# A state-space stage whose causal convolution of x runs with tokens on the partitions

## The chip, the cores and the metric

One core of one Trainium2 chip runs the whole program as a single launch. The metric is device time in microseconds (us); lower is better. The engines are TensorE (PE, with its weight loads PEld), VectorE (DVE), ScalarE (ACT), GpSimd (POOL) and SyncE (SP); copies run on 16 DMA engines. SBUF and PSUM tiles have 128 partitions.

## What is computed

The reference is a two-layer decoder trunk over 256 tokens of width 2048: latent attention, a squared-ReLU MLP, a Mamba-2 state-space mixer, and a second MLP. Everything is float32. Only the mixer is changed. Cut to what matters:

```python
zxbcdt = h @ w_in                                  # 256 x 10304
z, xbc, dt = split(zxbcdt, [4096, 4096 + 6144])    # xbc = x (4096) | B (1024) | C (1024)
xbc = silu(causal_depthwise_conv(xbc, conv_w, conv_b))   # 4 taps along the tokens, per channel
xs, b_in, c_in = split(xbc, [4096, 5120])          # 8 groups x 8 heads x 64 | 8 x 128 | 8 x 128
y = ssd_chunked_scan(xs, softplus(dt + dt_bias), a, b_in, c_in)   # one chunk of 256 tokens
y = (y + d_skip * xs) * silu(z)
y = y * rsqrt(mean(y * y over the group) + eps) * norm_g
x = x + y @ w_out
```

The convolution is out[s] = b + w3 v[s] + w2 v[s-1] + w1 v[s-2] + w0 v[s-3] for each channel, with zeros ahead of token 0.

## The kernel before

Every large product is float32 split in two halves. A unit of weights, 128 x 1024, is loaded into `wraw` by SP (six buffers). ACT copies it, rounded, to `wh` (`halves`, L103) and DVE subtracts to `wl` (L104), four buffers each. The products of a unit are 12 matmuls of 128 x 512 (`products`, L362 to L364). The loads run six units ahead of the products and the splits three (`flow.ahead`), so the split of unit j+4 needs the buffers that unit j gives up.

`ssm_plan` lists the units of the state-space stage in the order of `SSM_ORDER`. A step is a block of x, z, B or C: 8 units, whose result is 256 tokens x 512 channels in two PSUM banks with the tokens on the partitions. An output step "o" is 4 units for each of its four column blocks. TensorE's order is exactly the order in which the program text issues its instructions. On the other engines a list scheduler chooses the order. Small work between the units is timed by a clock in the code: `when(us, fn)` puts a function in a list, and `move(us)` advances the clock by 2.72 a unit and runs what is due; `small` also keeps such pieces apart.

x blocks 0 to 7 are the 8 head groups. `x_done` handles a finished one. `evac` copies its two banks to SBUF on ACT, scaled by the norm factor (L1117). `conv` then works in two halves of 256 channels. Four transposes (L1128) put the channels on the partitions and the tokens along the free axis. ACT forms tap 3 and the bias (L1135), DVE adds the other taps as shifted reads of the same PSUM bank, six instructions per half (L1138), and ACT applies Silu (L1139). `back` transposes the result to tokens on partitions again (L1257, twice four transposes per group), ACT copies it to `xtm` (L1260), and DVE, POOL and `across` prepare the operands of the chunk product: `xd` = x dt, a copy weighted by the decay to the chunk's middle (`xh`, `xl`), and x times the skip factor. `heads(g)` loads the decay rows (`cm`), takes exponentials and issues the group's 32 + 32 small matmuls in `product`. `gate` multiplies with silu(z), normalises and transposes (`turn`) to `yT`, which the output steps read. B and C blocks go through the same `conv` and stay with channels on the partitions.

DMAs are issued by SP, which processes its list in order, and by ACT where the code says `nc.scalar.dma_start`. A DMA that ACT issues stands in ACT's instruction order.

Of the kernel before, what the change touches and what calls it, by code (L numbers as in the profile page):

```python
# [20 lines left out]
F32 = mybir.dt.float32  # L21
# [3 lines left out]
ALU = mybir.AluOpType  # L25
# [205 lines left out]
class Trunk:  # L231
# [849 lines left out]
    def ssm_body(self, sp, dp, gain):  # L1081
# [16 lines left out]
        def small(us, fn, gap=2.6):  # L1098
            at[1] = max(at[0] + us, at[1] + gap)
            when(at[1] - at[0], fn)  # L1100
# [8 lines left out]
        heads_of = lambda v: v.rearrange("p (h f) -> p h f", h=8)  # L1109
        spread = lambda v, g: v[:, 8 * g:8 * g + 8].unsqueeze(2).to_broadcast([P, 8, 64])  # L1110
        diagonal = lambda: cst[:, C_TRI:C_TRI + P]

        def evac(accs):
            ev = []
            for t in range(2):
                e = self.scratch()
                nc.scalar.activation(e, accs[t], AF.Copy, scale=rs[t])  # L1117
                ev.append(e)
            return ev
# [38 lines left out]
        def cb_group(g):  # L1158
            B, C = fm["B", g // 4][:, g % 4], fm["C", g // 4][:, g % 4]
            b = self.ps(self.sm, "sm")  # L1160
            nc.tensor.matmul(b[:, 0:256], B[:, 0:P], C, start=True, stop=True)
            nc.tensor.matmul(b[:, 256:384], B[:, P:256], C[:, P:256], start=True, stop=True)
            at[0] += 0.65
            t = sp.tile([P, 2, P], F32, name=f"cb{g}")
            far[g] = sp.tile([P, 2, P], F32R, name=f"cf{g}")
            for i in range(2):
                nc.vector.tensor_tensor(t[:, i], b[:, 2 * i * P:2 * i * P + P], diagonal(), ALU.mult)
            self.split_out(far[g][:, 0], far[g][:, 1], b[:, P:256])
            cb[g] = t
# [20 lines left out]
        def dt_chain(b):  # L1190
# [50 lines left out]

            small(15, cums)

        def x_done(g, accs):
            fmx = [None, None]
            ev = evac(accs)
            xg[g], xd[g] = [None, None], [None, None]

            def dst(j, a):
                fmx[j] = a  # L1250
                return a

            def back(t):
                b = self.ps(self.sm, "sm")
                for k in range(4):
                    o = (k % 2) * 256 + t * P
                    nc.tensor.transpose(b[:, k * P:(k + 1) * P], fmx[k // 2][:, o:o + P], self.ident)  # L1257
                at[0] += 0.45
                x = sp.tile([P, 512], F32, tag="xtm", name=f"xtm{g}_{t}", bufs=XTM)
                nc.scalar.activation(x, b, AF.Copy)  # L1260
                w = sp.tile([P, 512], F32, tag="xd", name=f"xd{g}_{t}", bufs=XD)
                nc.vector.tensor_tensor(heads_of(w), heads_of(x), spread(dt[:, t], g), ALU.mult)
                xg[g][t], xd[g][t] = x, w
                if t == 0:
                    xw = self.scratch()
                    nc.gpsimd.tensor_tensor(heads_of(xw), heads_of(x), spread(edge[:, 0], g), ALU.mult)
                    xh = sp.tile([P, 512], F32R, tag="xh", name=f"xh{g}", bufs=1)
                    xl = self.s2.tile([P, 512], F32R, tag="s2", name=self.name("s2"))
                    self.split_out(xh, xl, xw)
                    small(8, lambda: across(xh, xl))  # L1270
                nc.gpsimd.tensor_tensor(heads_of(x), heads_of(x), spread(cst[:, C_DSK:C_DSK + 64], g), ALU.mult)
                if t:
                    waiting.append(g)
                    if len(waiting) == 1:
                        heads(g)

            def across(xh, xl):
                b = self.ps(self.sm, "sm")
                nc.tensor.matmul(b, far[g][:, 0], xh, start=True, stop=False)
                nc.tensor.matmul(b, far[g][:, 1], xh, start=False, stop=False)  # L1280
                nc.tensor.matmul(b, far[g][:, 0], xl, start=False, stop=True)
                at[0] += 0.7
                w = self.scratch()
                nc.vector.tensor_tensor(heads_of(w), heads_of(b), spread(edge[:, 1], g), ALU.mult)
                nc.gpsimd.tensor_tensor(xg[g][1], xg[g][1], w, ALU.add)

            def after():
                small(10, lambda: back(0))
                small(10, lambda: back(1))

            conv(ev, 4 * g, dst, after)

        def heads(g):

            cm = []
            for i in range(4):
                m = sp.tile([P, 2, 2, P], F32, tag="cm", name=f"cm{g}_{i}", bufs=4)
                nc.sync.dma_start(m.rearrange("p a t n -> p (a t n)"), cumD[4 * g + i:4 * g + i + 1].to_broadcast([P, 2 * S]))
                cm.append(m)

            def exponent(i):
                for k in range(2):
                    for t in range(2):
                        h = 8 * g + 2 * i + k
                        nc.scalar.activation(cm[i][:, k, t], cm[i][:, k, t], AF.Relu, bias=cumT[:, t, h:h + 1], scale=-1.0)

            def decay():
                for m in cm:
                    nc.scalar.activation(m, m, AF.Exp, scale=-1.0)
                scores = cb[g][:, 0:2].rearrange("p t n -> p (t n)").unsqueeze(1).to_broadcast([P, 2, 2 * P])  # L1310
                for m in cm:
                    v = m.rearrange("p a t n -> p a (t n)")
                    nc.vector.tensor_tensor(v, v, scores, ALU.mult)
                small(10, product)

            def product():
                y = [self.ps(self.yp, "y") for t in range(2)]
                for t in range(2):
                    for i in range(8):
                        o = slice(i * 64, (i + 1) * 64)  # L1320
                        for r in (slice(0, 64), slice(64, 128)):
                            nc.tensor.matmul(y[t][r, o], cm[i // 2][:, i % 2, t, r], xd[g][t][:, o], start=True, stop=True)
                at[0] += 1.8
                at[1] = max(at[1], at[0])
                for t in range(2):
                    nc.vector.tensor_tensor(xg[g][t], xg[g][t], y[t], ALU.add)
                waiting.pop(0)
                if waiting:
                    heads(waiting[0])

                def done():
                    ready.add(g)
                    gate(g)

                when(2, done)

            begin = 24 if g == 1 else 0
            for i in range(4):
                when(begin + 3 + 2.2 * i, lambda i=i: exponent(i))
            when(begin + 11, decay)  # L1340
# [9 lines left out]
        def gate(g):  # L1350
            if g not in ready or g not in ws:
                return
            ng = self.gain_tile(d["sng"][g])
            ssq = self.stat(2)
            for t in range(2):
                x = xg[g][t]
                nc.gpsimd.tensor_tensor(x, ws[g][t], x, ALU.mult)
                self.square_sum(x, ssq[:, t:t + 1])
            r = self.rsqrt(ssq, 2, 512)
            yT[g] = (self.ktile(self.k4), self.ktile(self.k4))  # L1360
            for t in range(2):
                nc.vector.scalar_tensor_tensor(ws[g][t], xg[g][t], r[:, t:t + 1], ng, ALU.mult, ALU.mult)

            def turn(t):
                sl = slice(t * P, (t + 1) * P)
                b = self.ps(self.sm, "sm")
                for j in range(4):
                    nc.tensor.transpose(b[:, j * P:(j + 1) * P], ws[g][t][:, j * P:(j + 1) * P], self.ident)
                at[0] += 0.45
                self.split_out(yT[g][0][:, :, sl], yT[g][1][:, :, sl], b.rearrange("p (k n) -> p k n", k=4))  # L1370

            lag = 14 if g == 1 else 10
            small(lag, lambda: turn(0))
            small(lag, lambda: turn(1))
            small(lag + 2, lambda: gated.add(g))

        done = {"B": lambda i, a: bc_done("B", i, a), "C": lambda i, a: bc_done("C", i, a), "x": x_done, "z": z_done}
        accs = None
        for tok in ssm_plan():
# [40 lines left out]


XTM, XD = 6, 4


def ssm_plan():
    out = []
    for step in SSM_ORDER:
# [7 lines left out]
        else:  # L1435
# [2 lines left out]


X_AT = (1, 2, 3, 3)  # L1440
SSM_ORDER = ["B0", "dt0", "C0", "x0", "x1", "B1", "C1", "z0", "z1", "x2", "x3", "o0", "z2", "z3", "x4", "x5", "o1",
             "z4", "z5", "x6", "x7", "o201", "z6", "z7", "o223"]


B12 = "raw"
# [195 lines left out]
```

## Time and profile before

| | |
|---|---|
| median of 3 runs | 2306.25 us (2305.49 to 2308.09) |
| profiled execution, its own time | 2306.98 us |
| its span, first to last instruction | 2305.2 us |
| PE, DVE, ACT, POOL busy | 2294.9, 1854.1, 1432.4, 182.7 us |
| granted TensorE clock, mean | 1.000 |
| state-space stage, projections and scan | about 957 to 1581 us of the span |
| in that stretch of 624 us: PE, DVE, ACT busy | 623.62, 428.15, 386.35 us |
| in that stretch: DMA engines' share, rate | 0.61, 192 GB/s |

PE's busy time is the union of its matmuls, which overlap; one unit of 12 matmuls takes 2.72 us from start to start. In rows of groups the columns are: source line, engine, operation, output <- inputs, shape, count | busy us, mean ns of one | idle us of the engine ahead of it and what ended that.

### The profile page before, as it was taken

Reading aid. Unit: us, or ns where it says so; the run is one execution under the profiler, and the core shown is the slowest. Engines: PE = TensorE matmul, PEld = TensorE weight load, DVE = VectorE, ACT = ScalarE, POOL = GpSimd, SP = SyncE. Lnnn points to the kernel's source line nnn. Section 1 sums busy time; section 2 is a strip of 40 time slices with the busy share of each in tenths; the row PEclk is TensorE's granted clock in tenths of the full one; section 3 lists DMA queues with packets and bytes.
Section 4 is the critical chain, followed back from the end, with each engine's and each line's share of the span. In section 5 each row is a group of like instructions: output and inputs, shape, how many; then the busy total and the mean of one; then the engine's idle time right before and its main releaser. Section 6 shows DMA issues by size and latency. Waiting matters only on the chain.

```text
span 2305.2 us, 30566 instructions
## 1 busy us (share of the span) xinstructions
PE 2294.9 (100%) x11065; PEld 1905.9 (83%) x11065; DVE 1854.1 (80%) x2180; ACT 1432.4 (62%) x1986; POOL 182.7 (8%) x223
## 2 busy tenths in 40 slices
PE   9999999999999999999999999999999999999999
PEld 7888888888888888888888888888888888888887
DVE  7776697999899897677677676766989889889895
ACT  7775465566666656576656566565666656666663
POOL 1430000000000000001010111110000000000000
PEclk9999999999999999999999999999999999999999
DMA  8444687887887877655566656566687788787874
GB/s 320 146 132 151 205 233 240 265 240 247 265 244 248 267 215 241 197 184 182 187 198 193 207 177 214 187 193 201 203 260 231 251 266 249 239 270 240 250 229 161
DMA packets 146102, 508.68 MB, mean 221 GB/s; under 512 B 16480, under 2 KB 17184, under 8 KB 145952
## 3 DMA queue, kind: packets, MB, share of 16 engines
q1 hardware_dynamic: 137664, 477.30, 62.8%
q0 software_dynamic: 8064, 29.36, 7.7%
q8 instruction: 87, 1.43, 0.2%
q14 instruction: 63, 0.52, 0.1%
q10 hardware_dynamic: 224, 0.07, 0.0%
HBM read 504.51 MB, written 2.16 MB: 220 GB/s over the span
## 4 chain that ended last, share of the span: by engine, by line
PE 97%; issue 1%; DVE 1%; DMA 0%; ACT 0%; POOL 0%; SPq 0%; DVEq 0%; ACTq 0%; POOLq 0%
PE yp L363 9%; PE yp L364 9%; PE yp L362 9%; PE acc L362 8%; PE acc L364 8%; PE acc L363 8%; PE st L363 8%; PE st L364 8%; PE st L362 8%; PE acc L345 3%; PE acc L341 3%; PE acc L342 3%; PE sm L326 2%; PE a L341 1%; PE kv L341 1%
## 5 line engine op out<-in xcount | busy, mean ns | idle before, releaser
L104 DVE TENSOR_TENSOR wl<-wraw,wh 128x1024 fp32r<-128x1024 f32 (+2 forms) x818 | 991.6, 1226 | 307.3 <-ACT wh L103 298.0
L103 ACT ACTIVATE wh<-wraw 128x1024 fp32r<-128x1024 f32 (+2 forms) x818 | 858.0, 1053 | 574.8 <-PE yp L364 178.2
L363 PE MATMUL yp<-wl,k 128*128 128x512 f32 x896 | 348.9, 389 | 1.0 <-DVE wl L104 1.0
L362 PE MATMUL yp<-wh,k 128*128 128x512 f32 x896 | 349.8, 390 | 0.0
L364 PE MATMUL yp<-wh,k 128*128 128x512 f32 x896 | 348.8, 389 | 0.0
L362 PE MATMUL acc<-wh,xt 128*128 128x512 f32 x704 | 279.3, 397 | 0.0
L363 PE MATMUL acc<-wl,xt 128*128 128x512 f32 x704 | 274.4, 390 | 0.4 <-DVE wl L104 0.4
L364 PE MATMUL acc<-wh,xt 128*128 128x512 f32 x704 | 274.7, 390 | 0.0
L103 ACT ACTIVATE wh<-wrx 128x1024 fp32r<-128x1024 f32 x168 | 177.9, 1059 | 136.4 <-PE yp L364 109.5
L104 DVE TENSOR_TENSOR wl<-wrx,wh 128x1024 fp32r<-128x1024 f32 x168 | 204.0, 1220 | 36.6 <-ACT wh L103 36.3
L363 PEld LDWEIGHTS yp<-wl,k 128*128 128x128 f32 x896 | 168.3, 188 | 36.3 <-DVE wl L104 1.9
L364 PEld LDWEIGHTS yp<-wh,k 128*128 128x128 f32 x896 | 168.2, 188 | 35.0
L362 PEld LDWEIGHTS yp<-wh,k 128*128 128x128 f32 x896 | 168.3, 188 | 34.6
L362 PE MATMUL st<-wh,xt 128*128 128x512 f32 x448 | 176.8, 395 | 0.0
L363 PE MATMUL st<-wl,xt 128*128 128x512 f32 x448 | 174.8, 390 | 0.0
L364 PE MATMUL st<-wh,xt 128*128 128x512 f32 x448 | 174.8, 390 | 0.0
L364 PEld LDWEIGHTS acc<-wh,xt 128*128 128x128 f32 x704 | 132.1, 188 | 28.1
L363 PEld LDWEIGHTS acc<-wl,xt 128*128 128x128 f32 x704 | 132.4, 188 | 27.1 <-DVE wl L104 1.2
L362 PEld LDWEIGHTS acc<-wh,xt 128*128 128x128 f32 x704 | 132.3, 188 | 26.1 <-issue 0.2
L199 POOL DMA_DIRECT2D wrx<-mi x56 | 49.0, 876 | 1140.8 <-DVE wl L104 988.6
L362 PE MATMUL st<-wh,sN 128*128 128x512 f32 x336 | 132.3, 394 | 0.0
L364 PE MATMUL st<-wh,sN 128*128 128x512 f32 x336 | 130.9, 390 | 0.0
(318 smaller groups left out, 3558.4 us busy)
## 6 DMA issues: line engine op xcount, KB each, us to landing
wraw<-mi SPq DMA_DIRECT2D x256, 512.0 KB, 5.2
wraw<-mo SPq DMA_DIRECT2D x256, 512.0 KB, 5.2
wraw<-si SPq DMA_DIRECT2D x160, 512.0 KB, 4.4
wraw<-so SPq DMA_DIRECT2D x64, 512.0 KB, 4.1
wrx<-mi SPq DMA_DIRECT2D x56, 512.0 KB, 5.0
wrx<-mi POOLq DMA_DIRECT2D x56, 512.0 KB, 8.0
wraw<-wo SPq DMA_DIRECT2D x32, 512.0 KB, 3.9
wraw<-ukv SPq DMA_DIRECT2D x16, 512.0 KB, 4.5
```

The lines of the kernel that those rows point to most:

```text
L103: self.last = nc.scalar.activation(h[:, v], raw[:, v], AF.Copy)
L104: nc.vector.tensor_tensor(lo[:, v], raw[:, v], h[:, v].bitcast(F32), ALU.subtract)
L199: nc.gpsimd.dma_start(st["b11"].tile, quarter(d, 1, 0), accum_op=ALU.add)
L326: self.nc.tensor.transpose(b[:, j * P:(j + 1) * P], src[:, j * P:(j + 1) * P], self.ident)
L341: nc.tensor.matmul(accs[t][:, :n], ah, wh[:, q, :], start=first and kt + q == 0, stop=False)
L342: nc.tensor.matmul(accs[t][:, :n], al, wh[:, q, :], start=False, stop=False)
L345: nc.tensor.matmul(accs[t][:, :n], lhs(kt + q, t)[0], wl[:, q, :], start=False, stop=en and q == nk - 1)
L362: nc.tensor.matmul(b, ah, wh, start=first and q == 0, stop=False)
L363: nc.tensor.matmul(b, ah, wl, start=False, stop=False)
L364: nc.tensor.matmul(b, al, wh, start=False, stop=last and q == 1)
```

## The change

B and C keep the old way. For x there are no transposes. `x_begin` copies a finished block into one tile `ev` (partitions = tokens, two token halves, 512 channels). For each half of 256 channels `shifted` issues six DMAs from ACT. For a shift m = 1, 2, 3 one copies 128 - m partitions of both token halves to `ex`, m partitions lower, and a second copies the m partitions that cross from the first 128 tokens to the second. `weighted` then runs on DVE: all three shifted copies times their taps in one 128 x 1536 instruction, and five 128 x 512 instructions for the unshifted tap, the bias and the sums. ACT's Silu writes `xtm`. The taps come as rows broadcast over the partitions (`cx`, one buffer, 640 KB, SP queue, 16 loads). `ev` and `ex` exist once, so the halves of all groups run one after the other through `line`; `LAG` holds the code's clock distances. `finish` does what `back` did after its copy. The order of the blocks is new, the special delays of group 1 are gone, the `cf` tiles share six buffers, and the SBUF scratch of software DMAs is 1024 bytes instead of 4096.

```diff
+        ex, ev, tap = sp.tile([P, 3, 2, 256], F32, name="ex"), sp.tile([P, 2, 512], F32, name="ev"), {}
+        line = []
+        nc.gpsimd.memset(ex[0:3, :, 0], 0.0)
...
-            far[g] = sp.tile([P, 2, P], F32R, name=f"cf{g}")
+            far[g] = sp.tile([P, 2, P], F32R, tag="cf", name=f"cf{g}", bufs=6)
...
+        def taps(k):
+            if k < 2 * GROUPS:
+                w = sp.tile([P, 5, 256], F32, tag="cx", name=f"cx{k}", bufs=1)
+                nc.sync.dma_start(w.rearrange("p a n -> p (a n)"), d["cx"][k:k + 1].to_broadcast([P, 5 * 256]))
+                tap[k] = w
+
         def x_done(g, accs):
-            ev = evac(accs)
...
-            def back(t):
-                    nc.tensor.transpose(b[:, k * P:(k + 1) * P], fmx[k // 2][:, o:o + P], self.ident)
...
-            conv(ev, 4 * g, dst, after)
+            line.append((g, accs))
+            if len(line) == 1:
+                x_begin(g, accs)
+
+        def x_begin(g, accs):
+            for t in range(2):
+                nc.scalar.activation(ev[:, t], accs[t], AF.Copy, scale=rs[t])
+
+            def shifted(j):
+                v = ev[:, :, j * 256:(j + 1) * 256]
+                for m in range(1, 4):
+                    nc.scalar.dma_start(ex[m:, m - 1], v[:P - m])
+                    nc.scalar.dma_start(ex[:m, m - 1, 1], v[P - m:, 0])
+                when(LAG[0], lambda: weighted(j))
+
+            def weighted(j):
...
+                def one():
+                    tt(ex, ex, w[:, 1:4].unsqueeze(2).to_broadcast([P, 3, 2, 256]), ALU.mult)
+                def two():
+                    tt(v, v, both(0), ALU.mult)
+                    tt(v, v, both(4), ALU.add)
+                def three():
+                    taps(2 * g + j + 1)
+                    tt(ex[:, 0], ex[:, 0], ex[:, 1], ALU.add)
+                    tt(v, v, ex[:, 2], ALU.add)
+                def four():
+                    tt(v, v, ex[:, 0], ALU.add)
+                    for t in range(2):
...
+                        nc.scalar.activation(xg[g][t][:, j * 256:(j + 1) * 256], v[:, t], AF.Silu)
+                    if j == 0:
+                        when(LAG[1], lambda: shifted(1))
+                    else:
+                        when(LAG[2], finish)
+                        line.pop(0)
+                        if line:
+                            x_begin(*line[0])
+
+                for i, fn in enumerate((one, two, three, four)):
+                    when(LAG[4] * i, fn)
...
-            begin = 24 if g == 1 else 0
+            begin = 0
...
-            lag = 14 if g == 1 else 10
+            lag = 10
...
+LAG = (6,0,8,14,2.6)
...
-SSM_ORDER = ["B0", "dt0", "C0", "x0", "x1", "B1", "C1", "z0", "z1", "x2", "x3", "o0", "z2", "z3", "x4", "x5", "o1",
-             "z4", "z5", "x6", "x7", "o201", "z6", "z7", "o223"]
+SSM_ORDER = ["B0", "dt0", "C0", "x0", "z0", "x1", "z1", "B1", "x2", "C1", "o001", "x3", "o023", "z2", "x4", "z3", "x5", "o101", "z4", "x6", "z5", "x7", "o123", "z6", "o201", "z7", "o223"]
...
-    nc = bacc.Bacc("TRN2", target_bir_lowering=False, num_devices=1, dynamic_dma_scratch_size=4096)
+    nc = bacc.Bacc("TRN2", target_bir_lowering=False, num_devices=1, dynamic_dma_scratch_size=1024)
```

How the change moves instructions shows best at x block 0. In rows of an order, a name's last number is the tile's running number, and the brackets list the semaphores that the instruction waits for (DMAHW0 to DMAHW7 are set by DMAs, which share these eight).

ACT before, from the end of x block 0: the two copies out of PSUM, the next weight split, and other work until the transposed half is ready.

```order
L1117 ACTIVATE s_688_9384<-acc_9165,rs_160 128x512 [waits PE_49]
L1117 ACTIVATE s_689_9386<-acc_9166,rs_160 128x512 [waits PE_49]
L103 ACTIVATE wh_9401<-wraw_9303 128x1024 [waits DMAHW5_49]
L315 ACTIVATE cf_9392<-sm_9388 128x128 [waits DVE_49,PE_49]
L1305 ACTIVATE cm_1_9583<-cm_1_9583,cumT 128x128
```

ACT now at the same place:

```order
L1261 ACTIVATE ev<-acc_9170,rs_160 128x512 [waits PE_49]
L1261 ACTIVATE ev<-acc_9171,rs_160 128x512 [waits PE_49]
L1267 DMA ex<-ev 1x16x16 [waits DMAHW5_49,Activation_49]
L1266 DMA ex<-ev 127x2x256 [waits DMAHW6_49,Activation_49]
L1266 DMA ex<-ev 126x2x256 [waits DMAHW7_49]
L1267 DMA ex<-ev 2x256 [waits DMAHW0_49]
L1266 DMA ex<-ev 125x2x256 [waits DMAHW1_49]
L1267 DMA ex<-ev 3x256 [waits DMAHW2_49]
L315 ACTIVATE cf_9401<-sm_9397 128x128 [waits DVE_49,PE_49]
L103 ACTIVATE wh_9410<-wraw_9308 128x1024
L103 ACTIVATE wh_9429<-wraw_9335 128x1024 [waits PE_49]
```

Six DMAs now stand between the copies out of PSUM and the next weight split.

DVE before, in the convolution of the same block: the weight splits `wl` alternate with shifted reads of PSUM that wait for ACT or for DVE itself.

```order
L104 TENSOR_TENSOR wl_9402<-wraw_9303,wh_9401 128x1024 [waits DMAHW5_49,Activation_49]
L316 TENSOR_TENSOR cf_9392<-sm_9388,cf_9392 128x128 [waits Activation_49]
L104 TENSOR_TENSOR wl_9435<-wraw_9330,wh_9434 128x1024 [waits DMAHW7_49,DVE_49,Activation_49]
L1138 SCALAR_TENSOR_TENSOR s_694_9422<-sm_9417,cst,s_694_9422 128x255 [waits Activation_49]
L1138 SCALAR_TENSOR_TENSOR s_694_9422<-sm_9417,cst,s_694_9422 128x254 [waits DVE_49]
L1313 TENSOR_TENSOR cm_0_9581<-cm_0_9581,cb_9324 128x512 [waits DMAHW2_49,Activation_49]
L1138 SCALAR_TENSOR_TENSOR s_694_9422<-sm_9417,cst,s_694_9422 128x253 [waits DVE_49]
```

DVE now:

```order
L104 TENSOR_TENSOR wl_9411<-wraw_9308,wh_9410 128x1024 [waits DMAHW6_49,Activation_49]
L1276 TENSOR_TENSOR ex<-ex,cx_8749 128x1536 [waits DMAHW5_49,DMAHW6_49,DMAHW2_49,DMAHW7_49,DMAHW1_49,DMAHW0_49]
L104 TENSOR_TENSOR wl_9430<-wraw_9335,wh_9429 128x1024 [waits DVE_49,Activation_49]
L1279 TENSOR_TENSOR ev<-ev,cx_8749 128x2x256
L104 TENSOR_TENSOR wl_9450<-wraw_9371,wh_9449 128x1024 [waits DVE_49,Activation_49]
L1280 TENSOR_TENSOR ev<-ev,cx_8749 128x2x256 [waits DVE_49]
L1284 TENSOR_TENSOR ex<-ex 128x512
L1285 TENSOR_TENSOR ev<-ev,ex 128x2x256 [waits DVE_49]
```

The instruction at L1276 waits for all six copies, and the weight splits of the next units stand behind it. There are 16 of these, one for each half of each group. Between ACT's place of the 127-partition copy and this instruction DVE has one weight split in 4 of the 16 cases, two in 10 and three in 2.

More of the change, by code (lines that the diff above doesn't have):

```diff
@@ L1242, in dt_chain @@
             small(15, cums)
+        def taps(k):
[3 more added lines that the diff above has]
+                tap[k] = w
         def x_done(g, accs):
-            fmx = [None, None]
-            ev = evac(accs)
+            line.append((g, accs))
+            if len(line) == 1:
+                x_begin(g, accs)
+        def x_begin(g, accs):
@@ L1247, in x_done @@
             xg[g], xd[g] = [None, None], [None, None]
-            def dst(j, a):
-                fmx[j] = a
-                return a
-            def back(t):
[L1254 to L1275, printed above, removed]
@@ new lines, in x_begin @@
+            for t in range(2):
[7 more added lines that the diff above has]
+            def weighted(j):
+                tt = nc.vector.tensor_tensor
+                v, w = ev[:, :, j * 256:(j + 1) * 256], tap[2 * g + j]
+                both = lambda i: w[:, i].unsqueeze(1).to_broadcast([P, 2, 256])
+                def one():
[11 more added lines that the diff above has]
+                        if j == 0:
+                            xg[g][t] = sp.tile([P, 512], F32, tag="xtm", name=f"xtm{g}_{t}", bufs=XTM)
+                        nc.scalar.activation(xg[g][t][:, j * 256:(j + 1) * 256], v[:, t], AF.Silu)
+                    if j == 0:
+                        when(LAG[1], lambda: shifted(1))
[6 more added lines that the diff above has]
+                    when(LAG[4] * i, fn)
@@ new lines, in finish @@
+            def finish():
+                x = xg[g]
+                for t in range(2):
+                    w = sp.tile([P, 512], F32, tag="xd", name=f"xd{g}_{t}", bufs=XD)
+                    nc.vector.tensor_tensor(heads_of(w), heads_of(x[t]), spread(dt[:, t], g), ALU.mult)
+                    xd[g][t] = w
+                    if t == 0:
+                        xw = self.scratch()
+                        nc.gpsimd.tensor_tensor(heads_of(xw), heads_of(x[0]), spread(edge[:, 0], g), ALU.mult)
+                        xh, xl = (self.s2.tile([P, 512], F32R, tag="s2", name=self.name("s2")) for _ in range(2))
+                        self.split_out(xh, xl, xw)
+                        small(LAG[3], lambda: across(xh, xl))
+                    nc.gpsimd.tensor_tensor(heads_of(x[t]), heads_of(x[t]), spread(cst[:, C_DSK:C_DSK + 64], g), ALU.mult)
+                waiting.append(g)
+                if len(waiting) == 1:
+                    heads(g)
@@ L1285, in across @@
                 nc.gpsimd.tensor_tensor(xg[g][1], xg[g][1], w, ALU.add)
-            def after():
-                small(10, lambda: back(0))
-                small(10, lambda: back(1))
-            conv(ev, 4 * g, dst, after)
+            shifted(0)
         def heads(g):
@@ L1375, in gate @@
             small(lag + 2, lambda: gated.add(g))
+        taps(0)
         done = {"B": lambda i, a: bc_done("B", i, a), "C": lambda i, a: bc_done("C", i, a), "x": x_done, "z": z_done}
@@ L1617 @@
     a["sidt"] = narrow(wi[:, 10240:])
+    cx = np.concatenate([f(ssm_conv_w)[0][::-1, :4096], f(ssm_conv_b)[0][None, :4096]]).astype(np.float32)
+    a["cx"] = np.ascontiguousarray(cx.reshape(5, 16, 256).transpose(1, 0, 2)).reshape(16, 5 * 256)
     a["so"] = pieces(f(ssm_w_out)[0])
```

## The prediction

> **What bounds the kernel now.** I read the page's busy table first, then busy time in the stretch of the state-space stage, then the waits in that stretch, then the chain that ended last.
>
> ```profile
> PE 2294.9 (100%) x11065; PEld 1905.9 (83%) x11065; DVE 1854.1 (80%) x2180; ACT 1432.4 (62%) x1986; POOL 182.7 (8%) x223
> 957.00:1581.00 624.00, 623.62 (x3320) 516.77 (x3319) 428.15 (x539) 386.35 (x586) 71.33 (x65) 1.00 0.61 192
> DVE wl L104 <- ACT wh L103: 170.7, 131, 6.0
> ACT wh L103 <- PE acc L364: 162.6, 111, 3.6
> ```
>
> The second row is the stage: length, busy PE, PEld, DVE, ACT and POOL, granted clock, DMA share, GB/s. PE idles 0.38 of 624 us there, so any work taken from PE is time gained, if the others keep up. The two waits show that they do: the weight split on DVE waits for ACT, and ACT waits for PE to give a buffer back. The supply of weights stands at its limit of four buffers, ahead of PE.
>
> ```profile
> 957.11 0.23 PE acc L362
> ...
> 973.45 3.83 PE sm L1176 x32
> 977.28 0.23 PE acc L362
> ...
> 980.03 0.44 PE sm L1128 x4
> 980.47 0.23 PE acc L362
> ...
> 983.23 0.44 PE sm L1128 x4
> ```
>
> These rows of the chain (start, length, what) give the prices on PE. From 957.11 to 973.45 six units pass, 2.72 us each. Four transposes take 0.44 us, and the unit between two such fours lasts 983.23 - 980.47 = 2.76 us, so each four also costs the unit behind it some 0.03.
>
> **The change part by part.** First, the transposes of x.
>
> ```profile
> L1128 PE MATMUL sm<-cst,s 128*128 128x128 f32 x96 | 14.3, 272 | 0.0
> L1257 PE MATMUL sm<-cst,s 128*128 128x128 f32 x64 | 9.8, 276 | 0.0
> ```
>
> All 64 at L1257 go. Of the 96 at L1128, x has 8 blocks of 8, so 64 go and 32 stay for B and C. That is 128 transposes, 32 fours at 0.47 us: 15.0 us off PE, all on the path. The products are the same in number, and the new order of blocks can win at most the 0.38 us of idle time. What it may lose I bound by 5 us either way and take as zero, because the waits for small matmuls are short in this stage.
>
> Second, DVE and ACT.
>
> ```profile
> L1138 DVE SCALAR_TENSOR_TENSOR s<-sm,cst,s 128x255 f32<-128x255 f32 (+1 forms) x144 | 65.6, 477 | 2.4 <-ACT s L1135 0.6
> L104 DVE TENSOR_TENSOR wl<-wraw,wh 128x1024 fp32r<-128x1024 f32 (+2 forms) x818 | 991.6, 1226 | 307.3 <-ACT wh L103 298.0
> L1326 DVE TENSOR_TENSOR xtm<-xtm,y 128x512 f32<-128x512 f32 x16 | 10.3, 680 | 0.0
> L1135 ACT ACTIVATE s<-sm,cst 128x256 f32<-128x256 f32 x48 | 26.0, 551 | 1.4 <-DVE s L1138 1.4
> L1117 ACT ACTIVATE s<-acc,rs 128x512 f32<-128x512 f32 x24 | 15.7, 683 | 5.3 <-PE acc L364 5.3
> L103 ACT ACTIVATE wh<-wraw 128x1024 fp32r<-128x1024 f32 (+2 forms) x818 | 858.0, 1053 | 574.8 <-PE yp L364 178.2
> L1139 ACT ACTIVATE s<-s 128x512 f32<-128x512 f32 x16 | 10.0, 625 | 0.6 <-DVE s L1138 0.3
> L1260 ACT ACTIVATE xtm<-sm 128x512 f32<-128x512 f32 x16 | 9.4, 589 | 6.2 <-PE sm L1257 6.2
> L1139 ACT ACT_TABLE_LOAD x5: 1283/1283/1283, 987.6 to 1095.8; - x5
> L1226 ACTq DMA_DIRECT2D cumD<-s x1: 504/504/504, 1004.6 to 1004.6; - x1
> ```
>
> DVE loses 96 of the 144 at L1138, 96 x 0.477 = 46 us. It gains per half one instruction of 1536 elements, about 1.23 + (1.23 - 0.68) = 1.77 us by the rows for 1024 and 512, and five of 512: 1.77 + 5 x 0.68 = 5.17 us. Sixteen halves are 83 us, so DVE grows by 37: 465 of some 609 us, still only 76%. ACT loses 32 at L1135 (18 us) and the 16 Silus and 16 copies of x (19), and gains 32 Silus of 256 columns (0.55 each, as at L1135, 18), 18 table loads of 1.28 us by its new order (23), and 96 DMA issues (48, by the 0.504 us of the one issue with that row): some 52 us net, 438 of 609. Neither becomes a bound by its sum. The cover is the idle time of the waits above.
>
> Third, the copies, where it is decided. `one` (L1276) waits for six copies. Behind it on DVE stand the weight splits, and PE waits for those. I work out from what landing time L of the 127-partition copy that wait reaches PE. Let PE end the last unit j of an x block at time 0. Splits up to j+3 are done. ACT copies out (2 x 0.69) and issues a small DMA and the 127 one (2 x 0.5), so it is under way at 2.4 and lands at 2.4 + L. The splits of j+4 and j+5 are done by about 8. `one` then needs 1.77 and the split of j+6 1.23 after the landing, so it is ready at 5.4 + L. PE needs it after five more units and one matmul, at 13.8. PE waits L - 8.4. With one split between copy and `one` it is L - 5.7, with three L - 11.2. The order has 4, 10 and 2 of these: together 16 L - 129 once L is above 11.2, nothing below 5.7, and between them 15 us, all that was gained, at about L = 8.7 (4 x 3.0 + 10 x 0.3).
>
> What is L? No copy of before has 127 partitions, so it is bounded from the rows of DMAs, those of the stage first.
>
> ```profile
> q1 hardware_dynamic: 35646, 119.28, 60.9%
> gb<-sng SPq DMA_DIRECT2D x6, 256.0 KB, 2.9
> cm<-cumD SPq DMA_DIRECT2D x32, 256.0 KB, 6.0
> ...
> DMA packets 146102, 508.68 MB, mean 221 GB/s; under 512 B 16480, under 2 KB 17184, under 8 KB 145952
> wraw<-mi SPq DMA_DIRECT2D x256, 512.0 KB, 5.2
> ...
> pos<-pos SPq DMA_DIRECT2D x1, 1.0 KB, 8.2
> ```
>
> The first three are of the stage; the columns of an issue are count, size and us to landing. One engine moved 119.28 MB / (0.609 x 16 x 624 us) = 19.6 KB in a us. A 256 KB load, 16.4 KB on each engine, lands in 2.9 us at best, of which 0.8 is moving and 2.0 is fixed.
>
> Lower end: the copies are spread over all 16 engines as every load is. The three long ones are 378 rows of 2 KB, 48 KB an engine, 2.5 us; with one weight load in the way (32.8 KB, 1.7) L = 6.2, near the 6.0 of the `cm` loads. Upper end: rows are dealt to the engines in equal shares. The listing of all issues (its first and last row are shown) has 1014 DMAs, and 16480 packets are short; 1014 x 16 + 256 small data packets is exactly 16480, so each DMA so far closed on 16 engines. All have 64 or 128 partitions, which 16 divides. 127 is prime, so equal shares mean one engine: 127 x 2 KB / 19.6 = 13.3 us, and L = 15.3. In equal shares 126 rows go to 14 engines (9 rows, 0.9 us) and 125 to 5 (25 rows, 2.6 us). They stand in the same line on that engine, so all have landed at 18.8. With four weight loads in between (6.7) it is 25.5.
>
> I take the equal shares, because all 1014 DMAs show them and none shows a remainder, and L = 18.8, since 19.6 KB/us was measured amid the weight loads. The Trainium skill, DMA: Bandwidth & Descriptors, section "Why a DMA increments its semaphore by 16 and not by 1", has the same rule: the largest number up to 16 that divides the slowest dimension, and one engine for 127 partitions; no run here shows it yet, and by it the sum stays as it is. So PE waits 16 x 18.8 - 129 = 172 us; with 15.3 it is 116, with 25.5 it is 279.
>
> The long waits might cost clock too; the granted clock is 1.00 in the row of the stage, where PE never pauses, so the sum has no such term. The Trainium skill, TensorE: Matmul & The Clock Gate, Part 1, says that after about 3.4 us of idling the array runs at half rate for about as long; 16 such starts would add an estimated 27 us, which no trace of before can show.
>
> Fourth, what is small. The tap loads, 16 x 640 KB, and the copies, 16 x 774 KB, add 23 MB to the stage's 119: 61% becomes 73% at most on average, hidden by loads six units ahead. On SP a tap load waits until DVE has passed L1280 (one buffer), and weight loads queue behind it. They are needed more than five units, 13.6 us, later and land in under 6, so I cost it at nothing; without that cover it is the third rival. POOL keeps its instructions. The smaller scratch concerns the 56 accumulating DMAs of the MLPs:
>
> ```profile
> POOL wrx L199 <- DVE wl L104: 988.6, 52, 39.6
> wrx<-mi POOLq DMA_DIRECT2D x56, 512.0 KB, 8.0
> ```
>
> POOL waits 988.6 us for DVE ahead of them, 19 us a time, while one lands in 8.0: few are under way together, and I cost it at nothing; were each to wait for the one ahead, up to 8 us would be hidden under those 19.
>
> The sum: 2306.98 us of the profiled execution (0.03% above the median of 2306.25) - 15.0 + 172 = 2464 us, from 2408 to 2571 by the ends of L.
>
> **The rivals.** (1) The copies are spread like loads, with a remainder on some engine. L is about 6.2, only four halves wait, 0.5 us each, and the kernel comes to 2307 - 15 + 2 = 2294, faster. For it speaks that every DMA so far used all 16 engines; against it, that none had a remainder. It decides below L = 8.7. (2) The copies are spread, but wait their turn among the weight loads, at a DMA share of 0.61 to 0.73, so that L is 8.3 to 9. PE then waits 4 x 2.6 to 4 x 3.3 + 10 x 0.6, 10 to 19 us: 2302 to 2311, within 0.2% (4.6 us), about what a measurement of this kernel can tell from no change. (3) The copies are quick, but SP stands at the tap load until DVE is through, and the weight loads behind it come late. At 2 us for each of 16 it gives 2294 + 32 = 2326, slower. Against it: in the stage's list of waits no weight split waits for a load, so the lead of six units is free.
>
> **How the numbers follow.** Equal shares 0.72; (1) 0.19; (2) 0.05; (3) 0.04. Slower by over 0.2% is the first and the last, 0.76, the same 0.05, faster 0.19. The time is that of the likeliest, 2464, whose own range is 2408 to 2571. Leaving out rival (1) and the edges of the first together would be more than 2 in 10, so the range begins at 2290 and ends at 2560, which leaves out the longest L alone.
>
> **What would show it.** In the changed profile: no L1257, 32 at L1128. The copies ex<-ev of 127 partitions take 15 to 25 us to land, those of 126 and 125 less or as long. DVE idles ahead of L1276 for copies, 16 times, some 10 to 17 us each, and PE loses about 170 us in the stage to splits (L104) that come late; DVE busy is 37 us more, and the MLPs last as before. Wrong it is if these copies land in 6 us or less, if DVE arrives at L1276 so late that they have landed, or if PE waits in this stage for weights' loads or for the small matmuls' operands instead.

## The result, and the profile after

The changed kernel takes 2509.55 us (median of 4 runs, 2499.19 to 2513.55) against 2306.48 us for the kernel before: 1.0873 times as long, 95% interval 1.0838 to 1.0907. The profiled execution took 2511.66 us with a span of 2509.8 us.

The busy table of the page after (us, share of the span, count):

```profile
PE 2328.0 (93%) x10937; PEld 1915.0 (76%) x10937; DVE 1877.7 (75%) x2180; ACT 1431.4 (57%) x1972; POOL 215.6 (9%) x224
```

PE has 128 matmuls fewer, and its busy time is still 33.1 us longer than before. Span less busy is the time in which PE stands: 10.3 us before, 181.8 now, 171.5 more. The two make the whole difference of the spans, 171.5 + 33.1 = 204.6 us. The same kernel after in three stretches (length, busy PE, PEld, DVE, ACT, POOL, granted clock, DMA share, GB/s):

```profile
0.00:957.00 957.00, 951.82 (x4468) 792.58 (x4469) 799.30 (x1022) 605.25 (x917) 85.14 (x127) 1.00 0.73 228
957.00:1785.00 828.00, 656.22 (x3201) 526.42 (x3200) 453.60 (x539) 386.22 (x573) 103.78 (x66) 0.89 0.55 172
1785.00:2507.00 722.00, 719.96 (x3271) 595.97 (x3269) 624.77 (x620) 439.97 (x483) 26.69 (x32) 1.00 0.77 236
```

All of it is in the state-space stage, 828 us where there were 624, with a clock of 0.89 where it was 1.00. The waits of that stage after (engine, line, what it waited for: us in all, times, longest):

```profile
DVE wl L104 <- ACT wh L103: 291.5, 64, 17.9
PEld acc L362 <- ACT wh L103: 160.4, 16, 11.9
PE acc L362 <- ACT wh L103: 153.8, 16, 11.5
ACT wh L103 <- issue: 138.7, 13, 16.1
ACT wh L103 <- DMA ex<-ev: 66.5, 5, 14.1
```

PE waits 16 times, once for each half of a group, for ACT's `wh`. ACT itself waits for "issue", which is no other engine. What stands in ACT's list shows in its timeline after, at the first x block (start, length, what):

```profile
1028.03 0.59 ACTq L1267 DMA_DIRECT2D ex<-ev  x1
1028.71 9.09 ACTq L1266 DMA_DIRECT2D ex<-ev  x2
1037.84 0.98 ACTq L1267 DMA_DIRECT2D ex<-ev  x1
1038.86 0.84 ACTq L1266 DMA_DIRECT2D ex<-ev  x1
1039.74 1.37 ACTq L1267 DMA_DIRECT2D ex<-ev  x1
1041.21 0.28 ACT L315 ACTIVATE cf<-sm 128x128 fp32r<-128x128 f32 x1 [12.60 <-DMA ex<-ev]
...
1055.98 0.72 ACTq L1266 DMA_DIRECT2D ex<-ev  x1
1058.82 12.61 ACTq L1267 DMA_DIRECT2D ex<-ev  x2
```

The six issues take 13 us of ACT, from 1028.03 to 1041.11. Most of that is in one of them, and the chain of waits of the kernel after tells which:

```profile
1028.71 1.27 ACTq L1266
1029.98 0.04 issue
1030.02 7.78 ACTq L1266
...
1039.74 7.45 DMA ex<-ev
1047.19 0.04 DVEq L1276
```

The issue of the 127-partition copy takes 1.27 us. The issue behind it, that of the 126-partition copy, takes 7.78. In the second half of the group, where a small copy of L1267 follows the one of 127, the pair of 12.61 us holds the pause. The issues of the two lines after (count, shortest/median/longest in ns, first and last start) show that a few are long and the rest are not:

```profile
L1266 ACTq DMA_DIRECT2D ex<-ev x48: 712/844/11039, 1028.7 to 1671.4; - x48
L1267 ACTq DMA_DIRECT2D ex<-ev x48: 554/748/14974, 1028.0 to 1672.9; - x48
```

In all 16 halves the issue right behind the copy of 127 is the held one, for 7.6 to 15.0 us. In the chain, the last copy has landed at 1047.19, 18.5 us after the start of the issue of the first long one.

Two groups after (columns as before):

```profile
L1131 PE MATMUL sm<-cst,s 128*128 128x128 f32 x32 | 4.8, 272 | 0.0
L1276 DVE TENSOR_TENSOR ex<-ex,cx 128x1536 f32<-128x1536 f32 x16 | 29.4, 1837 | 40.4 <-DMA ex<-ev 38.1 <-DMA wraw<-si 2.3
```

32 transposes are left. DVE stands 40 us in all ahead of `one` (L1276), 2.5 a time. By the prediction this was the place of the whole loss, at 10 to 17 us a time.

What a pause does to PE behind it, in PE's timeline after:

```profile
1036.34 0.39 PE L364 MATMUL acc<-wh,xt 128*128 128x512 f32 x1
1042.49 0.80 PE L362 MATMUL acc<-wh,xt 128*128 128x512 f32 x1 [5.76 <-ACT wh L103]
...
1044.76 0.63 PE L362 MATMUL acc<-wh,xt 128*128 128x512 f32 x1
1045.19 0.63 PE L363 MATMUL acc<-wl,xt 128*128 128x512 f32 x1
...
1048.60 0.59 PE L362 MATMUL acc<-wh,xt 128*128 128x512 f32 x1
...
1050.88 0.39 PE L362 MATMUL acc<-wh,xt 128*128 128x512 f32 x1
1051.11 0.39 PE L363 MATMUL acc<-wl,xt 128*128 128x512 f32 x1
```

After 5.76 us of standing, matmuls start 0.43 us apart; from 1050.65 on it is 0.23 again. From 1042.49 to 1048.60 twelve matmuls took 6.1 us, of which 0.46 is a second wait; at 0.227 they take 2.7. So about 2.9 us are lost to the clock at this pause. The stage has 16 stretches in which the granted clock is 0.50, one for each half of a group. The first of them and the sum of all (columns as in the three stretches above):

```profile
1038.79:1049.03 10.24, 6.08 (x13) 4.09 (x13) 3.18 (x3) 7.39 (x16) 0.00 (x0) 0.50 0.33 105
...
sum 177.48, PE 75.91 PEld 54.37 DVE 47.55 ACT 90.28 POOL 6.21; mean PE 4.74 PEld 3.40 DVE 2.97 ACT 5.64 POOL 0.39
```

The clock falls while PE still stands and stays low for 10.2 us. PE is busy for 75.9 us in these stretches; by the spacing of 0.43 us for 0.227 the clock costs some 36 us of them, an estimate for all 16 pauses.

### The profile page after: what moved, and what is told of

It is laid out like the page before. It is cut to its first block, busy times and chain, and to the rows that moved or that the text cites. A ratio compares the mean times of both kernels' runs of the same rounds, so it can differ in the third digit from the quotient of the medians.

```text
span 2509.8 us, 30439 instructions
## 1 busy us (share of the span) xinstructions
PE 2328.0 (93%) x10937; PEld 1915.0 (76%) x10937; DVE 1877.7 (75%) x2180; ACT 1431.4 (57%) x1972; POOL 215.6 (9%) x224
## 4 chain that ended last, share of the span: by engine, by line
PE 77%; DMA 7%; ACTq 5%; DVE 4%; issue 4%; ACT 2%; POOL 1%; SPq 0%; DVEq 0%; POOLq 0%
PE yp L363 8%; PE yp L364 8%; PE yp L362 8%; PE st L363 7%; PE st L364 7%; PE st L362 7%; PE acc L363 5%; PE acc L364 5%; PE acc L362 5%; DMA ex<-ev 4%; ACTq L1266 3%; PE acc L345 3%; PE acc L341 3%; PE acc L342 3%; DVE wl L104 2%
## 5 line engine op out<-in xcount | busy, mean ns | idle before, releaser
L362 PE MATMUL acc<-wh,xt 128*128 128x512 f32 x704 | 290.4, 413 | 117.8 <-ACT wh L103 117.8
L363 PE MATMUL acc<-wl,xt 128*128 128x512 f32 x704 | 286.4, 407 | 14.3 <-DVE wl L104 14.3
L364 PE MATMUL acc<-wh,xt 128*128 128x512 f32 x704 | 283.4, 403 | 0.0
L362 PEld LDWEIGHTS acc<-wh,xt 128*128 128x128 f32 x704 | 138.7, 197 | 151.5 <-ACT wh L103 122.7
L363 PEld LDWEIGHTS acc<-wl,xt 128*128 128x128 f32 x704 | 138.4, 197 | 52.0 <-DVE wl L104 24.1
L364 PEld LDWEIGHTS acc<-wh,xt 128*128 128x128 f32 x704 | 137.8, 196 | 29.1
L362 PE MATMUL st<-wh,sN 128*128 128x512 f32 x336 | 132.3, 394 | 0.0
L363 PE MATMUL st<-wl,sN 128*128 128x512 f32 x336 | 131.1, 390 | 0.0
```

The costliest lines, as they stand in the source:

```text
L362: nc.tensor.matmul(b, ah, wh, start=first and q == 0, stop=False)
L363: nc.tensor.matmul(b, ah, wl, start=False, stop=False)
L364: nc.tensor.matmul(b, al, wh, start=False, stop=last and q == 1)
```

## The experiments

Diffs are against the changed kernel unless said. Theory A is equal shares (a copy of 127 partitions runs on one DMA engine, and holds the next issue behind it), B the number of issues on ACT, C the late landing whoever issues. Each ratio is to runs of the kernel before on the same chip (medians 2306.5 to 2307.2 us), with its 95% interval.

**Cut the copy of 127 into 112 and 15.**

```diff
-                    nc.scalar.dma_start(ex[m:, m - 1], v[:P - m])
+                    for a, z in ((0, 112), (112, 127)) if m == 1 else ((0, P - m),):
+                        nc.scalar.dma_start(ex[m + a:m + z, m - 1], v[a:z])
```

> The copy of 127 partitions is cut in 112 and 15, everything else as in the changed kernel. Theory A (rows are dealt to the DMA engines in equal shares, so 127 rows run on one engine; behind them the next DMA that ACT issues is held for 9 to 13 us, ACT's weight splits stop and PE waits): the largest share on one engine is now 25 rows of the copy of 125, 50 packets, 2.6 us; ACT is held by 1 to 2 us at most, PE hardly waits, 2292 to 2302 us. Rival B (what costs is the number of DMAs that ACT issues, 0.7 to 0.8 us each, with the added table loads and DVE work): 16 more issues, 2510 to 2525 us. Rival C (the copies land late and DVE waits for them, wherever they are issued): 2292 to 2302 as A.

2361.55 us, ratio 1.0235 (1.0220 to 1.0250): 148 us of the 203 are gone by cutting one copy in two. The issues of the long copies of this kernel, and PE's wait for `wh` in the stage:

```profile
L1267 ACTq DMA_DIRECT2D ex<-ev x64: 658/872/1446, 1026.9 to 1532.7; - x64
...
PE acc L362 <- ACT wh L103: 18.0, 10, 4.5
PE acc L363 <- DVE wl L104: 23.2, 16, 4.5
```

No issue lasts over 1.45 us now. The copy of 127 alone makes the hold, and with it most of the loss. Yet 54 us are left, 60 over what A expected, so A is not all. DVE still waits 22.7 us in all for copies at `one`, and the larger of PE's two waits is now the one for `wl`, which DVE makes.

**Cut all three long copies at 112**, `for a, z in ((0, 112), (112, P - m))`, still on ACT.

> All three long copies are cut at row 112 (112+15, 112+14, 112+13). Theory A: largest share 7 rows, 14 packets; 2290 to 2300 us, equal to the kernel with one cut or up to 3 us better. Rival B: 48 more issues of 0.75 us than in the changed kernel, 2520 to 2545 us. Rival C: as A.

2375.54 us, 1.0302 (1.0285 to 1.0319): 14 us more than with one cut, for 32 more issues. The theory of landing time gave a gain or nothing. PE waits for `wh` twice as long as with one cut, and less for `wl` (14.9 us). The row of `wh` in this kernel:

```profile
PE acc L362 <- ACT wh L103: 34.0, 13, 4.9
```

The wait for `wh` grows with the issues on ACT; the time that is left also depends on how even the copies are.

**Issue the six uncut copies from SP.**

```diff
-                    nc.scalar.dma_start(ex[m:, m - 1], v[:P - m])
-                    nc.scalar.dma_start(ex[:m, m - 1, 1], v[P - m:, 0])
+                    nc.sync.dma_start(ex[m:, m - 1], v[:P - m])
+                    nc.sync.dma_start(ex[:m, m - 1, 1], v[P - m:, 0])
```

> The same six copies per half, uncut, but issued by SP instead of ACT. Theory A: ACT no longer stands still, SP does; the weight loads behind it have a lead of six units (some 16 us), so PE is not starved by them at once, and the remaining price is DVE's wait at the 1536-element product for the landing: 2330 to 2460 us, clearly below 2510, with DVE's wait for copies far above the 38 us of the changed kernel. Rival B: about 2440 to 2470 us (72 us of issue time gone from ACT). Rival C: 2500 to 2520 us, since the copies land no sooner.

2488.04 us (2 runs), 1.0784 (1.0763 to 1.0806). Waits in the stage of this kernel:

```profile
DVE ex L1276 <- DMA wraw<-si: 118.2, 9, 14.8
DVE ex L1276 <- DMA ex<-ev: 66.8, 5, 14.7
DVE ex L1276 <- DMA wraw<-so: 15.1, 1, 15.1
DVE ex L1276 <- DMA cm<-cumD: 14.4, 1, 14.4
PE acc L363 <- DVE wl L104: 148.4, 16, 13.3
```

The time lies above A's range and in that of neither rival. With ACT's list free, DVE waits 214.5 us ahead of `one`, 13.4 a time, and PE for the splits behind it: the place that the prediction gave, and nearly the size. (`one` waits on semaphores that other DMAs also set, hence the names of weight loads in the rows.) So the late landing costs nearly as much without ACT's hold; in the changed kernel that hold hides it, since it delays the next splits by as long. The hold itself is not gone. It has moved to SP:

```profile
L1267 SPq DMA_DIRECT2D ex<-ev x48: 573/760/9847, 1027.1 to 1660.0; - x48
```

In each of the 16 halves SP is held 7.4 to 9.9 us in the issue behind the copy of 127, and the copies behind that issue start as much later. So this kernel doesn't tell the copy's own time on one engine from the hold's share in the late landing.

**Long copies of 112 rows only**, issued by ACT, six a half. It leaves out the last 15, 14 and 13 rows, so its time alone counts; `ex` is cleared whole at the start.

```diff
-                    nc.scalar.dma_start(ex[m:, m - 1], v[:P - m])
+                    nc.scalar.dma_start(ex[m:m + 112, m - 1], v[:112])
```

> Leaves out the last 15, 14 and 13 rows of the three long copies, so each has 112 rows and 16 divides it; six issues per half as in the changed kernel. Theory A: 2289 to 2298 us, the price of everything in the change but the odd copies. Rival B: 2500 to 2515 us. Rival C: as A.

2329.74 us (2 runs), 1.0098 (1.0078 to 1.0118), where A gave 2289 to 2298. The issues take 0.5 to 1.2 us, none is held, PE waits 6.4 us for `wh` and 15.2 for `wl`, and the kernel is 23 us slower than before: with even copies this change still did not pay when ACT issued them.

**The copy of 127 in the kernel before**, once for each x block, read by nobody (diff against the kernel before; j is 0).

```diff
+        dm, dn = sp.tile([P, 2, 272], F32, name="dm"), sp.tile([P, 256], F32, name="dn")
...
+                nc.scalar.dma_start(dm[128 - 127:, :, 0:256], ev[j][:127].rearrange("p (a n) -> p a n", a=2))
```

> The kernel before with one added DMA per group, issued by ACT behind the two copies out of PSUM: 127 partitions x 2 x 256 of one of them to a tile that nobody reads (8 in all). No other DMA follows on ACT within the same group. Theory A (an odd copy runs on one engine for 13 us or more, and it is the next DMA on the same issuing engine that is held there): nothing on ACT is held, nobody waits for the copy, 2305 to 2315 us. Rival B (an issue of this kind costs the issuing engine itself 10 us): 2330 to 2380 us.

2307.48 us (8 runs), 1.0003 (0.9992 to 1.0013): nothing. Its packet row:

```profile
DMA packets 148144, 510.78 MB, mean 222 GB/s; under 512 B 16488, under 2 KB 19224, under 8 KB 147992
```

Before, 16480 packets were short, 16 for each of 1014 DMAs and 256 of data. The eight copies add 8, one each: a copy of 127 partitions runs on one engine.

**The same with a small copy of 3 rows right behind it** on ACT (`nc.scalar.dma_start(dn[:3], ev[j][P - 3:, 0:256])`).

> As the kernel before with the added copy of 127 partitions per group, and right behind it a second small DMA of 3 partitions x 256 on ACT, also read by nobody. Theory A: the small one is held 8 to 12 us in each of the 8 groups; ACT's split of the next unit is due within about 8 us of the end of the x block, so PE waits 3 to 6 us a time: 2330 to 2360 us. Rival B: as the kernel with the copy alone plus 5 us.

2351.84 us (2 runs), 1.0195 (1.0174 to 1.0215). Issue rows of the two copies:

```profile
L1250 ACTq DMA_DIRECT2D dm<-s x8: 729/731/1297, 1026.4 to 1521.8; - x8
L1251 ACTq DMA_DIRECT2D dn<-s x8: 7547/8292/8803, 1027.8 to 1522.6; - x8
```

The small copy holds ACT 8.3 us, and eight of them cost 45 us in a kernel that does nothing else differently. Where nobody waits for the copy of 127, only what follows it on the same queue makes it dear. It is no wait for a semaphore: three of the eight small copies wait for none, and for the other five it came at least 4 us before the hold ended. PE's busy time grows by 16.4 us here (2311.3 against 2294.9) though it waits only 28.2 us. One such place in PE's timeline of this kernel:

```profile
1037.94 0.50 PE L362 MATMUL acc<-wh,xt 128*128 128x512 f32 x1 [1.86 <-ACT wh L103]
1039.20 0.80 PE L363 MATMUL acc<-wl,xt 128*128 128x512 f32 x1 [0.76 <-DVE wl L104]
1039.80 0.63 PE L364 MATMUL acc<-wh,xt 128*128 128x512 f32 x1
```

Two pauses of 1.86 and 0.76 us with one matmul between them are enough for matmuls of 0.63 us, until 1042.4.

**All three cut, issued by POOL** (`nc.gpsimd.dma_start`, nine a half).

> The changed kernel with the three long copies cut at row 112 and all nine DMAs of a half issued by POOL instead of ACT. Theory A with the price of the issues (0.7 to 0.85 us of ACT's time each, six to nine in a row ahead of the next weight split, is what is left of the loss once no copy is odd): ACT keeps its splits in time, 2292 to 2306 us, at least as fast as before. Rival B (what is left is DVE's and ACT's added work and the new order, not the issues): 2325 to 2345 us as with the 112-row copies.

2357.54 us, 1.0228 (1.0209 to 1.0246), where A gave 2292 to 2306. Waits of the stage:

```profile
POOL ex L1268 <- ACT ev L1261: 130.0, 8, 70.1
DVE ex L1277 <- DMA ex<-ev: 75.6, 16, 7.9
DMA to landing us min/median/max: 1.6/6.2/8.6
```

The copies are even, but come late to `one` in all 16 halves. POOL does not reach the issues late: in the first half of each group it waits for ACT's copy out of PSUM and then issues at once. It is the landing that is late. The last row is that of the small copies (L1268), and `one` starts 5.8 to 7.1 us after the last issue, against 1.2 to 2.8 in the next kernel, where SP issues.

**Cut for m = 1 and 3, issued by SP**, eight a half: even copies and ACT's list free at once.

```diff
+                    for a, z in ((0, 112), (112, P - m)) if m != 2 else ((0, 126),):
+                        nc.sync.dma_start(ex[m + a:m + z, m - 1], v[a:z])
+                    nc.sync.dma_start(ex[:m, m - 1, 1], v[P - m:, 0])
```

> The changed kernel with the copy of 127 cut in 112 and 15 and that of 125 in 112 and 13 (126 is left whole), all issued by SP. Theory A with the price of the issues: ACT is free, SP stands 6 to 7 us per half but its loads lead by six units: 2292 to 2310 us. Rival B: 2325 to 2345 us.

2304.70 us (10 runs), 0.9991 (0.9982 to 1.0001). Both prices are gone: 183 us below the uncut copies on SP, 57 to 71 below the cut ones on ACT, and within A's 2292 to 2310. But no gain is left of the transposes. Waits of PE in the stage:

```profile
PE sm L1409 <- DVE s L1403: 8.5, 4, 4.4
PE acc L363 <- DVE wl L104: 0.9, 1, 0.9
```

PE waits 8.5 us for DVE ahead of the transposes that turn y. These stand 10 us behind their DVE work on the code's clock (`lag = 10`), so the next kernels move them.

**The same with `lag = 14`.**

> The kernel with cut copies issued by SP, and the transposes of the gated result (turn) placed 14 us behind the gate on the code's clock for every group instead of 10 (the kernel before had 14 for group 1 alone). In the run with 10 PE waited 8.5 us in all for the gate's DVE instruction ahead of these transposes, 3 to 4 times. If that wait is what keeps the gain of 15 us away, this gives 2293 to 2298 us; if the transposes only wait later or the other waits grow, 2302 to 2306 us.

2303.45 us (11 runs), 0.9987 (0.9978 to 0.9996), the fastest of all, by 0.13%, which is under the 0.2% that the prediction set as the least to tell. Had the turn's wait been all, it was to be 2293 to 2298; it lies in the other range, where other waits grow. The wait for the turn is gone, and PE waits 7.9 us, 5 times, for weight splits instead.

**The same with `lag = 16`.**

> As the kernel with 14, with 16 us. If the longest wait of 4.8 us is only covered by 16: 2292 to 2296 us, up to 2 us better than with 14; if 14 is enough, the same as that.

2310.98 us (11 runs), 1.0019 (1.0010 to 1.0027), slower than either expectation. PE waits 10.7 us for `wl` and 3.1 for `wh`.

**`lag = 14`, and `one` later after the copies**: `LAG = (9,0,8,14,2.6)` for `(6,0,8,14,2.6)`.

> The kernel with cut copies issued by SP and turn at 14 us, and the DVE part of a half placed 9 us behind its copies on the code's clock instead of 6. With 6, DVE waited 14.5 us in all for copies at the 1536-element product and PE 7.9 us for weight splits, at a granted clock of 0.99 in the stage. If the product placed too early is what is left: PE idles under 2 us in the stage and the time is 2293 to 2299 us. If DVE's larger work itself makes the splits late: 2301 to 2306 us.

2307.30 us (11 runs), 1.0000 (0.9991 to 1.0009). The stage and PE's wait in it:

```profile
957.00:1581.00 624.00, 611.92 (x3191) 503.30 (x3190) 461.00 (x539) 384.86 (x570) 94.19 (x65) 1.00 0.71 228
PE acc L363 <- DVE wl L104: 12.0, 11, 2.1
```

The clock is 1.00, so nothing is slowed. PE's work in the stage is 11.7 us less than before (623.62), and PE waits 12.0 us for splits. DVE is busy 461 us, where it was 428. That DVE's larger work is what makes the splits late is the likeliest reading, since moving `one` away from the copies did not help; no run takes DVE's work away alone.

**And with 8 in place of 9.**

> As the kernel with 9 us, with 8. If the early product is what is left, 2294 to 2301 us, between the kernels with 6 and with 9; otherwise 2301 to 2306 us.

2306.95 us (11 runs), 0.9997 (0.9988 to 1.0006), splits late by about as much. Both are 1 us above the range for DVE's larger work. Their intervals overlap that of `lag = 14`, so whether they lose its 3 us is open too.

The runs by span less PE busy (PE stands) and PE busy, from their pages:

| kernel | span us | PE busy | PE stands | clock |
|---|---|---|---|---|
| before | 2305.2 | 2294.9 | 10.3 | 1.000 |
| changed | 2509.8 | 2328.0 | 181.8 | 0.964 |
| uncut, SP | 2485.0 | 2318.2 | 166.8 | 0.965 |
| all cut, ACT | 2372.8 | 2313.5 | 59.3 | 0.988 |
| 127 cut, ACT | 2358.9 | 2307.6 | 51.3 | 0.990 |
| all cut, POOL | 2349.1 | 2299.5 | 49.6 | 0.993 |
| 112 rows, ACT | 2326.6 | 2295.7 | 30.9 | 0.995 |
| cut, SP | 2303.0 | 2284.6 | 18.4 | 0.999 |
| cut, SP, lag 14, `one` at 9 | 2305.5 | 2284.0 | 21.5 | 1.000 |

## Why the prediction was right, and where not

Slower was right, and 2511.66 us lies in the range. It is 47.7 us over the forecast of 2464. The chain of the loss was right in its first link, a copy of 127 partitions on one engine, and wrong in the next: PE waited for `wh`, not for the `wl` behind `one`. Point by point:

- **Transposes, -15.0 us.** The sign was right, the size too large by about 4: with the clock at 1.00, PE has 10.9 us less work in the whole kernel (2284.0 against 2294.9). Where the rest of the 0.47 us per four went is open.
- **DVE +37 us, ACT +52 us, neither a bound.** DVE's busy time grew by 23.6 us in the changed kernel and by 30 to 33 with the copies cut and issued by SP. The cover was there for the sum, not at each place: once the copies were cheap, PE stood 8 to 14 us for splits or, with `lag = 10`, for the turn, about what the transposes gave. ACT's busy time did not change (1431.4 against 1432.4), since issues are not counted in it. The 18 further table loads came (38 against 20).
- **Equal shares, one engine for 127 partitions.** Right: one short packet for each copy of 127 added to the kernel before. In the changed kernel 1168 short packets are new. 16 tap loads on 16 engines are 256, and the 16 pieces of the one-row copies are 256. The other 656 are 41 a half, which is 1 + 14 + 5 engines for the long copies and 16 + 2 + 3 for the small ones, as equal shares give. The Trainium skill, DMA: Bandwidth & Descriptors, section "Why a DMA increments its semaphore by 16 and not by 1", has this rule; the packet rows agree, of the changed kernel's page too:

```profile
DMA packets 161495, 531.66 MB, mean 212 GB/s; under 512 B 17648, under 2 KB 30528, under 8 KB 161344
```

- **L = 18.8 us.** 18.5 measured at the first half, and 17.8 to 22.1 over the 16 halves, from the start of the issue of 127 to that of `one`. But the way there was another: the next copies stood in ACT's hold, not only in the engine's line.
- **PE waits 172 us.** PE stood 171.5 us more, but by another wait. The step that failed is "16 L - 129", which lets ACT go on 0.5 us after each issue: ACT was held inside the issue behind the copy of 127, 7.8 us at the first half and up to 15.0 at the longest. The agreement is in part luck: with ACT free, the late landing comes near the same sum (156.5 us more standing for the uncut copies on SP, at the predicted place), and the two prices overlap.
- **96 issues at 0.504 us, covered by ACT's idle time.** Mis-sized. Where none is held they take 0.64 to 0.87 us each (medians), and six or more in a row delay `wh`: PE's wait for it is 6.4 us with 96 issues (112 rows), 18.0 with 112 and 34.0 with 144. Those kernels are 23, 54 and 68 us over the one before, which the evenness of the copies also moves; with even copies issued by SP nothing is left.
- **No term for the clock.** This is the error in the number. The prediction took the clock from the stage before (1.00), where PE never pauses. Against the 2284.0 us of PE work at full clock the changed kernel is busy 44 us longer; the 16 stretches at 0.50 make some 36 of these, the other 8 are open. The Trainium skill, TensorE: Matmul & The Clock Gate, Part 1, speaks of some 3.4 us at half rate after an idle window of as long, which made the estimate of 27 us. The trace agrees on the half rate (0.50); it lasted 10.2 us at the pause shown, 6.1 of them with PE busy, and 3.4 us (1039.1 to 1042.5) at the one of the kernel with the small copy.
- **New order, tap loads, SP, scratch, 0.** The stretches around the stage last as before, and with the copies even on SP the time is that of before. So together they cost no more than the 8 us that PE stands longer there (18.4 against 10.3).

Of the rivals, spreading with a remainder (2294) is refuted by the packets. Its time was not reached with copies that 16 divides either: it let the issues and DVE's work go free. Even copies on SP come to 2304.70, in the range of the rival whose copies wait their turn (2302 to 2311), but PE's wait there is mostly for the turn (8.5 us, against 0.9 for splits). SP's tap load (2326) did not show: with 128 further issues on SP the kernel takes 2304.70.

## What to carry to other kernels

Choose the partition counts of a copy so that 16 divides them, or cut it into such a part and a small rest (112 + 15 for 127): the one odd count cost 148 us here. Put a DMA where the next one on the same queue, and the engine that issues it, can wait; here ACT, which makes TensorE's weights, was the wrong issuer, and SP, with its loads six units ahead, a free one. And count each pause of TensorE at more than its length: here 172 us of pauses brought some 36 more by the clock.

## What the runs showed of the hardware

- A copy of 127 partitions, two pieces of 1 KB each, leaves its issuing engine after 0.7 to 1.3 us, but the next DMA of that queue, even one of 3 rows, is held 7.5 to 8.8 us in the issuing engine (7.6 to 15.0 on ACT in the changed kernel, 7.4 to 9.9 on SP). How much such a queue can take is not measured; that it fills is inferred from these times.
- The granted clock fell to 0.50 after 2.6 us of pauses with one matmul among them, not only after long ones, and stayed there 3.4 us; in the changed kernel it stayed 10.2 us at the pause shown.
- An issue from ACT that is not held takes 0.64 to 0.87 us here (medians), against the 0.504 us of the single one before.
